# Row normalization on one core: all scaling moved to VectorE, ScalarE left with the stores

## The chip, the cores and the metric

The kernel runs on one core of one Trainium2 chip. The metric is device time in microseconds (us). Before the change it was 317.7 us (median of 3 runs, 317.55 to 318.85). Each run comes with a state: it is slow when it lies over 1.5% above the fastest run of the same kernel. A page of the profile describes one profiled execution; its span is about 2 us shorter than the time of the same run. A ratio of two kernels is the mean time of the one's fast runs over that of the other's of the same rounds, so it is not quite the ratio of the medians that are quoted beside it. An interval is a 95% interval.

## The reference

```python
x: (32, 512, 1024) float32
sums = np.sum(np.abs(x), axis=-1, keepdims=True)
return (x / (sums + 1e-8)).astype(np.float32)
```

There are 16384 rows of 1024 numbers, 67.1 MB in and 67.1 MB out. Each number is read once and written once.

## The kernel before

The rows are cut into ten tiles of 12 rows a partition (6.29 MB each) and one of 8 (4.19 MB). Four buffers of 48 KB a partition rotate, so load 4 (counting from 0) cannot be issued until store 0 has landed. Loads are issued by SyncE, stores by ScalarE. Names are shortened in the cut below.

```python
R = 12
BUFS = 4
...
def normalize(x_tile, r0, k, kv):
    s = stats.tile([P, R], FP32)
    nc.vector.tensor_reduce(out=s[:, :k], in_=x_tile[:, r0 : r0 + k, :],
        axis=X, op=add, apply_absolute_value=True)
    nc.vector.tensor_scalar_add(out=s[:, :k], in0=s[:, :k], scalar1=EPS)
    inv = stats.tile([P, R], FP32)
    nc.vector.reciprocal(out=inv[:, :k], in_=s[:, :k])
    nc.vector.tensor_mul(                      # rows 0 .. kv-1 on VectorE
        out=x_tile[:, r0 : r0 + kv, :], in0=x_tile[:, r0 : r0 + kv, :],
        in1=inv[:, :kv].unsqueeze(2).to_broadcast([P, kv, d]))
    for r in range(kv, k):                     # the other rows on ScalarE
        row = x_tile[:, r0 + r, :]
        nc.scalar.activation(out=row, in_=row, func=Copy, scale=inv[:, r : r + 1])

for i, k in enumerate(rows):
    x_tile = sbuf.tile([P, R, d], FP32)
    nc.sync.dma_start(out=x_tile[:, :k, :], in_=piece(x_flat, i))
    normalize(x_tile, 0, k, k // 2)
    nc.scalar.dma_start(out=piece(out_flat, i), in_=x_tile[:, :k, :])
```

Of the kernel before, what the change touches and what calls it, by code (L numbers as in the profile page):

```python
# [1 line left out]

# [4 lines left out]

FP32 = mybir.dt.float32
EPS = 1e-8


@with_exitstack
def kernel(
    ctx: ExitStack,
    tc: tile.TileContext,
    x: bass.AP,
    out: bass.AP,
):
    nc = tc.nc
    P = nc.NUM_PARTITIONS  # L20

    x_flat = x.flatten_outer_dims()
    out_flat = out.flatten_outer_dims()
    n, d = x_flat.shape


    R = 12
    BUFS = 4
    per_partition = n // P
    assert n % P == 0  # L30
    rows = [R] * (per_partition // R)
    if per_partition % R:
        rows.append(per_partition % R)

    def piece(flat, i):
        a, k = P * sum(rows[:i]), rows[i]
        return flat[a : a + P * k, :].rearrange("(p r) d -> p r d", p=P)

    sbuf = ctx.enter_context(tc.tile_pool(name="sbuf", bufs=BUFS))
    stats = ctx.enter_context(tc.tile_pool(name="stats", bufs=4))  # L40

    def normalize(x_tile, r0, k, kv):

        s = stats.tile([P, R], FP32)
        nc.vector.tensor_reduce(  # L45
            out=s[:, :k],
            in_=x_tile[:, r0 : r0 + k, :],
            axis=mybir.AxisListType.X,
            op=mybir.AluOpType.add,
            apply_absolute_value=True,  # L50
        )
        nc.vector.tensor_scalar_add(out=s[:, :k], in0=s[:, :k], scalar1=EPS)  # L52
        inv = stats.tile([P, R], FP32)
        nc.vector.reciprocal(out=inv[:, :k], in_=s[:, :k])  # L54
        nc.vector.tensor_mul(  # L55
            out=x_tile[:, r0 : r0 + kv, :],
            in0=x_tile[:, r0 : r0 + kv, :],
            in1=inv[:, :kv].unsqueeze(2).to_broadcast([P, kv, d]),
        )
        for r in range(kv, k):  # L60
            row = x_tile[:, r0 + r, :]
            nc.scalar.activation(  # L62
                out=row,
                in_=row,
                func=mybir.ActivationFunctionType.Copy,
                scale=inv[:, r : r + 1],
            )

    with tc.manual_schedule():
        for i, k in enumerate(rows):  # L70
            x_tile = sbuf.tile([P, R, d], FP32)
            nc.sync.dma_start(out=x_tile[:, :k, :], in_=piece(x_flat, i))  # L72
            normalize(x_tile, 0, k, k // 2)
            nc.scalar.dma_start(out=piece(out_flat, i), in_=x_tile[:, :k, :])  # L74


# [1 line left out]
_INS = ['x']  # L78
_OUTS = [((32, 512, 1024), 'float32')]


# [23 lines left out]
```

## Time and profile before

| | before |
|---|---|
| time, median | 317.7 us |
| VectorE (DVE) busy | 212.4 us, 67% |
| ScalarE (ACT) busy | 69.0 us, 22% |
| DMA, mean over the span | 425 GB/s |
| VectorE's wait for loads, all tiles | 81.1 us |

These lines are from the page of the kernel before: the span, the busy time of each engine, and the busy share in 40 equal slices (a digit is tenths, 9 is 90% or more).

```profile
span 315.8 us, 227 instructions
...
DVE 212.4 (67%) x44; ACT 69.0 (22%) x65; POOL 0.2 (0%) x4
...
DVE  0069999998499079719944991797099449949300
...
DMA  8999999999999999999999999999999999999996
```

The reader is to see the row of DMA: it is full in every slice but the first and the last. Nothing that an engine saves can shorten this kernel unless it lets the DMA engines move the same bytes in less time.

The costliest groups of the kernel before (line, engine, operation, tile names, shapes, count; then busy time and mean ns of one; then idle time just before and what ended it):

```profile
L45 DVE TENSOR_REDUCE s<-x_tile 128x12 f32<-128x12288 f32 (+1 forms) x11 | 138.2, 12564 | 81.1 <-DMA x_tile<-in_x_dram 81.1
L62 ACT ACTIVATE x_tile<-x_tile,inv 128x1024 f32<-128x1024 f32 x64 | 67.7, 1135 | 207.6 <-DVE inv L54 207.6
L55 DVE TENSOR_TENSOR x_tile<-x_tile,inv 128x6144 f32<-128x6144 f32 (+1 forms) x11 | 70.0, 6364 | 0.4
```

The multiply is shared about equally: per tile 6.56 us on VectorE beside 6.34 us on ScalarE. VectorE waits 81.1 us for loads, so it has room.

The start of the timeline of the kernel before, merged (start, length, engine, line, operation): tile 0 is multiplied, and its store is issued.

```profile
31.81 6.34 ACT L62 ACTIVATE x_tile<-x_tile,inv 128x1024 f32<-128x1024 f32 x6 [12.13 <-DVE inv L54]
31.81 6.56 DVE L55 TENSOR_TENSOR x_tile<-x_tile,inv 128x6144 f32<-128x6144 f32 x1
38.28 12.95 DVE L45 TENSOR_REDUCE s<-x_tile 128x12 f32<-128x12288 f32 x1
38.45 0.37 ACTq L74 DMA_DIRECT2D out_dram<-x_tile  x1
```

The first store goes out at 38.45 us.

### The profile page before, as it was taken

To read this page: it belongs to the slowest core of one execution; us is meant where nothing else is said; L and a number is where in the kernel's file an instruction comes from. 1 tells how busy PE (TensorE), PEld (TensorE's weight loads), DVE (VectorE), ACT (ScalarE), POOL (GpSimd) and SP (SyncE) were. 2 spreads that over 40 slices of the span, in tenths; PEclk is the share of its full clock that TensorE was granted. 3 is DMA by queue.
4 is the path that set the end of the run, shared out by engine and by line. 5 is a ranking of instruction groups with operands and counts; after the bars stand their busy time and mean duration, and the time that the engine had idled before them with its cause. 6 is when DMAs were issued, how large, how long until landed. Compare 5 with 4: busy or idle time off the path is not lost.

```text
span 315.8 us, 227 instructions
## 1 busy us (share of the span) xinstructions
DVE 212.4 (67%) x44; ACT 69.0 (22%) x65; POOL 0.2 (0%) x4
## 2 busy tenths in 40 slices
DVE  0069999998499079719944991797099449949300
ACT  0010804308007000700440070007003400701300
POOL 0000000000000000000000000000000000000000
DMA  8999999999999999999999999999999999999996
GB/s 311 467 417 411 467 367 442 405 454 430 417 448 430 423 461 423 436 442 417 442 442 411 449 436 411 448 436 423 448 430 436 442 413 450 421 448 417 448 403 278
DMA packets 3169, 134.23 MB, mean 425 GB/s; under 512 B 352, under 2 KB 352, under 8 KB 352
## 3 DMA queue, kind: packets, MB, share of 16 engines
q1 hardware_dynamic: 1584, 67.11, 49.8%
q10 hardware_dynamic: 1584, 67.11, 49.1%
q14 instruction: 1, 0.01, 0.0%
HBM read 67.11 MB, written 67.11 MB: 425 GB/s over the span
## 4 chain that ended last, share of the span: by engine, by line
DMA 55%; DVE 25%; another core or an unknown queue 9%; ACT 4%; issue 0%; SPq 0%; DVEq 0%; ACTq 0%
DMA x_tile<-in_x_dram 41%; DVE s L45 19%; DMA out_dram<-x_tile 14%; DVE x_tile L55 6%; ACT x_tile L62 4%; DVE inv L54 0%; DVE s L52 0%; SPq L72 0%; DVEq L54 0%; ACTq L74 0%
## 5 line engine op out<-in xcount | busy, mean ns | idle before, releaser
L45 DVE TENSOR_REDUCE s<-x_tile 128x12 f32<-128x12288 f32 (+1 forms) x11 | 138.2, 12564 | 81.1 <-DMA x_tile<-in_x_dram 81.1
L62 ACT ACTIVATE x_tile<-x_tile,inv 128x1024 f32<-128x1024 f32 x64 | 67.7, 1135 | 207.6 <-DVE inv L54 207.6
L55 DVE TENSOR_TENSOR x_tile<-x_tile,inv 128x6144 f32<-128x6144 f32 (+1 forms) x11 | 70.0, 6364 | 0.4
L62 ACT ACT_TABLE_LOAD x1 | 1.3, 1283 | 18.4 <-DMA x_tile<-in_x_dram 18.4
L54 DVE RECIPROCAL inv<-s 128x12 f32<-128x12 f32 (+1 forms) x11 | 2.5, 226 | 0.9
L52 DVE TENSOR_SCALAR s<-s 128x12 f32<-128x12 f32 (+1 forms) x11 | 1.9, 173 | 0.4
L89 POOL MEMSET const-bfloat16-1.0<- 128x1 bf16 x1 | 0.1, 101 | 0.0
L89 POOL MEMSET const-uint8-127<- 128x1 uint8 x1 | 0.1, 101 | 0.0
L89 POOL MEMSET const-float32-0.0<- 128x1 f32 x1 | 0.1, 98 | 0.2 <-issue 0.2
L89 POOL MEMSET const-float32-1.0<- 128x1 f32 x1 | 0.1, 98 | 0.0
## 6 DMA issues: line engine op xcount, KB each, us to landing
x_tile<-in_x_dram SPq DMA_DIRECT2D x10, 6144.0 KB, 38.5
out_dram<-x_tile ACTq DMA_DIRECT2D x10, 6144.0 KB, 53.5
x_tile<-in_x_dram SPq DMA_DIRECT2D x1, 4096.0 KB, 33.7
out_dram<-x_tile ACTq DMA_DIRECT2D x1, 4096.0 KB, 19.5
```

Source lines behind the costliest of these rows:

```text
L45: nc.vector.tensor_reduce(out=s[:, :k], in_=x_tile[:, r0 : r0 + k, :], axis=mybir.AxisListType.X, op=mybir.AluOpType.add, apply_absolute_v ...
L52: nc.vector.tensor_scalar_add(out=s[:, :k], in0=s[:, :k], scalar1=EPS)
L54: nc.vector.reciprocal(out=inv[:, :k], in_=s[:, :k])
L55: nc.vector.tensor_mul(out=x_tile[:, r0 : r0 + kv, :], in0=x_tile[:, r0 : r0 + kv, :], in1=inv[:, :kv].unsqueeze(2).to_broadcast([P, kv, d]),)
L62: nc.scalar.activation(out=row, in_=row, func=mybir.ActivationFunctionType.Copy, scale=inv[:, r : r + 1],)
L89: nc = _bacc.Bacc("TRN2", target_bir_lowering=False, num_devices=1)
```

## The change

The intent is to drop the 64 small ScalarE instructions and the uneven split of work: one broadcast multiply per tile on VectorE, and ScalarE only issues stores.

```diff
-    def normalize(x_tile, r0, k, kv):
+    def normalize(x_tile, r0, k):
 ...
         nc.vector.tensor_mul(
-            out=x_tile[:, r0 : r0 + kv, :],
-            in0=x_tile[:, r0 : r0 + kv, :],
-            in1=inv[:, :kv].unsqueeze(2).to_broadcast([P, kv, d]),
+            out=x_tile[:, r0 : r0 + k, :],
+            in0=x_tile[:, r0 : r0 + k, :],
+            in1=inv[:, :k].unsqueeze(2).to_broadcast([P, k, d]),
         )
-        for r in range(kv, k):
-            row = x_tile[:, r0 + r, :]
-            nc.scalar.activation(...)
 ...
-            normalize(x_tile, 0, k, k // 2)
+            normalize(x_tile, 0, k)
```

More of the change, by code (lines that the diff above doesn't have):

```diff
@@ L55, in normalize @@
         nc.vector.tensor_mul(
-            out=x_tile[:, r0 : r0 + kv, :],
-            in0=x_tile[:, r0 : r0 + kv, :],
-            in1=inv[:, :kv].unsqueeze(2).to_broadcast([P, kv, d]),
-        )
-        for r in range(kv, k):
-            row = x_tile[:, r0 + r, :]
-            nc.scalar.activation(
-                out=row,
-                in_=row,
-                func=mybir.ActivationFunctionType.Copy,
-                scale=inv[:, r : r + 1],
-            )
+            out=x_tile[:, r0 : r0 + k, :],
+            in0=x_tile[:, r0 : r0 + k, :],
+            in1=inv[:, :k].unsqueeze(2).to_broadcast([P, k, d]),
+        )
     with tc.manual_schedule():
```

## The prediction

> What bounds the kernel now. The 16 DMA engines. The page's slices show them at 90% or more in every slice but the first and last, 134.23 MB at 425 GB/s over a span of 315.8 us. Loads and stores share them: in the timeline the tile period settles at 29.0 us (reduces begin at 112.19, 141.21, 170.26, ...), and 2 x 6.29 MB in 29.0 us is 434 GB/s. The Trainium skill, "DMA: Bandwidth & Descriptors", section "Where 436 GB/s comes from", gives 435 GB/s as the ceiling for one core; this trace agrees (434). VectorE is busy 67%, ScalarE 22%; VectorE waits 81.1 us for loads (waits view), 8.9 us per tile in the steady part. A store is issued about 53 us before it lands, though 6.29 MB take 29 us at half rate: some 25 us is queueing behind the store before.
>
> What changes. Removed: 64 ACTIVATEs of 1.13 us (67.7 us of ScalarE, 6.34 us per tile, beside VectorE's multiply of 6.56 us) and a hidden table load of 1.28 us. Added: VectorE multiplies 12288 instead of 6144 elements. The trace has 6557 ns for 6144 and 4425 ns for 4096 elements: 1.041 ns an element plus 0.16 us, so an estimated 12.95 us (8.69 us for the last tile), as much as the reduce. The Trainium skill, "VectorE: DVE Perf Modes", section "The perf-mode tier table", has fp32 tensor_tensor at one element a cycle at any size; the two sizes agree. VectorE's period per tile goes from 19.93 us (two unstalled tiles in the timeline) to about 26.35 us.
>
> Critical path. 26.35 is still below the DMA period of 29.0, so the extra 6.4 us per tile should come out of two slacks: VectorE's 8.9 us wait for a load, and the store's queueing. With four buffers a load waits for the store of four tiles ago; that store starts when the store queue reaches it, not when VectorE is done. The end is tight. VectorE begins at 18.35; if it never waits it ends at 18.35 + 10 x 26.35 + 17.9 = about 300 us (295 before). By then about 4 to 5 MB of stores should be left, and the last store (4.19 MB, 9.7 us at 434 GB/s, plus some 2 us to land) ends at about 312 to 316. Laid out by hand at 434 GB/s shared equally, before and after end within 1 us of each other. A VectorE period of 27 us would cost some 2 us, 28 about 12 us: the margin is thin, but the period follows from measured durations.
>
> Predicted: 318.2 us, 8 in 10 between 316.5 and 321.5. Faster by over 2%: 0.02; within 2%: 0.92; slower by over 2%: 0.06.
>
> What would show it. The 12288-element multiply at 12.9 to 13.0 us; VectorE 88 to 90% busy, its idle time before reduces down from 81 us to under 25, mostly the first load; ScalarE with no busy time; DMA still 9 in nearly all slices; median time from a store's issue to landing down from 53 us to 30 to 40; first store issued near 45 us, last near 300 us.
>
> What would make it wrong. The multiply slower than its two sizes say, or slowed by DMA traffic; a gap in the DMA engines near 75 us, when the four loads are done and the fifth waits for the first store; stores issued so late at the end that the engines idle; a time lower by over 2% would mean that DMA was not at its limit.

## More of the kernel before

The end of the kernel before in windows of 10 us (window, its length, busy time of each engine, granted clock, DMA share, GB/s):

```profile
290.00:300.00 10.00, 4.92 (x4) 4.27 (x4) 0.00 (x0) 1.00 1.02 442
300.00:310.00 10.00, 0.00 (x0) 0.00 (x0) 0.00 (x0) 1.00 0.97 419
310.00:320.00 10.00, 0.00 (x0) 0.00 (x0) 0.00 (x0) 1.00 0.28 119
```

The engines stay full until after 310 us and then stop together.

## The result, and the profile after

The changed kernel takes 325.15 us (median of 4 runs, 324.84 to 325.33) against 317.66 us; the ratio is 1.0226 (1.0201 to 1.0252). It is slower by 2.3%, and it lies outside the predicted range of 316.5 to 321.5 us.

The same lines of the changed kernel's page:

```profile
span 323.3 us, 134 instructions
...
DVE 280.2 (87%) x44; POOL 0.2 (0%) x4
...
DVE  0079999999999999999999999999599959999900
...
DMA  8999899999999999999999999999999999999792
...
L45 DVE TENSOR_REDUCE s<-x_tile 128x12 f32<-128x12288 f32 (+1 forms) x11 | 138.2, 12560 | 25.5 <-DMA x_tile<-in_x_dram 25.5
L55 DVE TENSOR_TENSOR x_tile<-x_tile,inv 128x12288 f32<-128x12288 f32 (+1 forms) x11 | 138.3, 12570 | 0.4
```

What VectorE does is nearly as predicted: one multiply costs as much as one reduce, and its wait for loads has shrunk from 81.1 to 25.5 us (under 25 was predicted, and 88 to 90% busy instead of 87). Of the 25.5 us, 18.0 are the first load; the other 7.5 us come late, in front of tiles 7, 8 and 9 (0.78, 3.29 and 3.44 us in the timeline). But for one 8 near 36 us, where the packets followed below show no idle engine, the DMA row has lost digits only at the end.

The timeline at the first store, and the last windows, of the changed kernel (the windows have no ScalarE column, since it is never busy):

```profile
31.49 12.96 DVE L55 TENSOR_TENSOR x_tile<-x_tile,inv 128x12288 f32<-128x12288 f32 x1
44.37 12.95 DVE L45 TENSOR_REDUCE s<-x_tile 128x12 f32<-128x12288 f32 x1
44.48 0.38 ACTq L66 DMA_DIRECT2D out_dram<-x_tile  x1
```

```profile
290.00:300.00 10.00, 9.90 (x4) 0.00 (x0) 1.00 1.06 457
300.00:310.00 10.00, 6.92 (x1) 0.00 (x0) 1.00 0.72 308
310.00:320.00 10.00, 0.00 (x0) 0.00 (x0) 1.00 0.78 336
320.00:325.00 5.00, 0.00 (x0) 0.00 (x0) 1.00 0.03 13
```

The first store is issued at 44.48 us instead of 38.45. At the end the DMA share is 0.72 and 0.78 where before it was 0.97 until the work ran out.

### Looking at the 16 DMA engines one by one

The page gives the mean of the 16 DMA engines. The trace also records each packet (queue, start, duration, bytes) and each engine's report that its part of a DMA has landed. The tables below are worked out from these records. A DMA of 128 partitions is spread over 16 engines, 8 packets of 48 KB each (one partition's run of 12 rows). The records do not name the engine, so I chained packets: one that starts where another ends belongs to the same engine. In the kernel before this gives 16 chains of exactly 176 packets, 88 loads and 88 stores; in the other kernels a few chains swap some packets where two ends coincide.

First and last of the 16 landings of a store, in us from the span's start:

```
                 before                    changed
store   issued  first   last  apart   issued  first   last  apart
0         38.5   70.9   73.6    2.7     44.5   76.1   80.2    4.1
1         58.4   99.9  102.6    2.8     70.8   97.8  106.7    8.9
3        103.4  157.9  160.7    2.8    123.5  157.7  166.0    8.3
6        190.4  244.9  247.6    2.7    202.4  243.0  255.4   12.4
9        277.4  303.5  305.0    1.5    289.2  304.9  312.7    7.8
10       295.2  313.2  314.7    1.5    307.0  317.9  322.4    4.5
```

Before, the 16 engines work in step. In the changed kernel some are up to 12.4 us behind others. The Trainium skill, "DMA: Bandwidth & Descriptors", section "Why a DMA increments its semaphore by 16 and not by 1", states that only the full count of 16 means that all data have landed. This trace agrees: load 10 was issued at 255.5 us, just after store 6's last landing at 255.4, and 12.5 us after its first. So a tile always waits for the slowest engine.

The engines that fall behind are not idle. Nearly every packet takes 1.815 us (27.1 GB/s an engine, 433 GB/s for 16). Some take longer. Call the time over 1.815 us extra. Summed up to the last packet's end and averaged over the engines:

```
                         before   changed   difference
last packet's end         314.2     322.1        +7.8
extra packet time           2.2       4.2        +2.0
idle time of engines        2.7       8.5        +5.8
```

The two differences add up to the whole loss, as they must: an engine has the same bytes to move in both kernels, and is otherwise slow or idle. Until 280 us no engine idles in either kernel except in the first 2 us. The idle time is at the end, where fast engines have nothing left to do: on twelve engines some 3 us before the last store, which VectorE hands over only at 307.0 us, and another 4.4 us between their end at 317.6 us and that of the slowest at 322.1.

Here is where the extra time starts. These are the first packets around store 0 on two engines of the changed kernel. L3.1 is load 3's packet 1, S0.0 is store 0's packet 0; the figure is the duration in us.

```
engine with 25 load packets ahead of its first store packet (4 of 16 engines; 2 look like this, on the other 2 load packets are slow as well):
L3.0 2.51 | S0.0 1.81 | L3.1 1.82 | S0.1 2.10 | L3.2 1.81 | S0.2 2.48 | L3.3 1.81 | S0.3 2.43 | L3.4 1.81 | S0.4 2.47 | L3.5 1.81 | S0.5 2.50 | L3.6 1.81 | S0.6 2.44
engine with 26 load packets ahead (12 of 16 engines):
L3.1 2.76 | S0.0 1.82 | L3.2 1.81 | S0.1 1.81 | L3.3 1.81 | S0.2 1.82 | L3.4 1.81 | S0.3 1.81 | L3.5 1.81 | S0.4 1.81 | L3.6 1.82 | S0.5 1.81
```

Both alternate between a load and a store packet. The Trainium skill, the same page, section "Queues, rings and completion order", states that each engine takes turns between its queues packet by packet, and these lines agree. But on the first engine, where store packet j follows load packet j of tile 3, the store packets take about 2.45 us; on the second, shifted by one packet, none does. In the kernel before, the engines have 22 or 23 load packets ahead, and store packets take 1.81 us on all 16.

### The profile page after: what moved, and what is told of

It reads as the page before. It is cut to its first block, busy times and chain, and to the rows that moved or that the text cites. A ratio compares the mean times of both kernels' runs of the same rounds, so it can differ in the third digit from the quotient of the medians.

```text
span 323.3 us, 134 instructions
## 1 busy us (share of the span) xinstructions
DVE 280.2 (87%) x44; POOL 0.2 (0%) x4
## 4 chain that ended last, share of the span: by engine, by line
DVE 62%; DMA 32%; issue 0%; SPq 0%
DVE x_tile L55 31%; DVE s L45 31%; DMA x_tile<-in_x_dram 17%; DMA out_dram<-x_tile 15%; DVE inv L54 1%; DVE s L52 0%; SPq L64 0%
## 5 line engine op out<-in xcount | busy, mean ns | idle before, releaser
L45 DVE TENSOR_REDUCE s<-x_tile 128x12 f32<-128x12288 f32 (+1 forms) x11 | 138.2, 12560 | 25.5 <-DMA x_tile<-in_x_dram 25.5
L55 DVE TENSOR_TENSOR x_tile<-x_tile,inv 128x12288 f32<-128x12288 f32 (+1 forms) x11 | 138.3, 12570 | 0.4
```

The lines of the kernel that those rows point to most:

```text
L55: nc.vector.tensor_mul(out=x_tile[:, r0 : r0 + k, :], in0=x_tile[:, r0 : r0 + k, :], in1=inv[:, :k].unsqueeze(2).to_broadcast([P, k, d]),)
```

## The experiments

Four theories were on the table at the start. T, mine after reading the traces: loads come late, engines are out of step, and VectorE, having no slack any more, waits. V: only the sum of VectorE's work matters. E: only the later last store matters. D: engines that are out of step cost the time by themselves, whatever VectorE does.

### Which tile matters

`split_first`, `split_middle` and `split_last` are the changed kernel with one tile split as before (tile 0, tile 5, the last). `vector_first` is the kernel before with one tile unsplit.

```diff
# split_first (0), split_middle (5), split_last (len(rows) - 1); the loop before, with
-            normalize(x_tile, 0, k, k // 2)
+            normalize(x_tile, 0, k, k // 2 if i == 0 else k)
# vector_first
+            normalize(x_tile, 0, k, k if i == 0 else k // 2)
```

> Changed kernel, but tile 0 is split between VectorE and ScalarE as before. Theory T (the fifth load waits for a late first store, the 16 DMA engines get out of step, loads come late, and VectorE, which has no slack, waits for them): the first store goes out at 38.5 instead of 44.5 us, stores' landings stay within 3 to 4 us from first to last engine instead of 8 to 12, load 9 lands near 257 instead of 262.7, time 317.5 to 320. Rival V (only the sum of VectorE's work matters): 325.1 minus 6.4, near 318.7, with no change of the landing spreads.

> Changed kernel, but only tile 5 (in the middle) is split. Theory T: VectorE is 6.4 us sooner with tile 5 but then waits for loads 7 to 9, which are as late as before (load 9 lands near 262 to 263); VectorE's waits after the first load rise from 7.5 to about 14 us, the time stays at 324 to 326. Rival V (sum of VectorE's work): near 318.7.

> Changed kernel, but only the last tile (8 rows) is split. It takes VectorE 4.3 us less, all of it after load 9's wait. Theory T: the loads are as late as in the changed kernel (load 9 at 262 to 263), the last store is issued at 302.7 instead of 307.0, time 320.5 to 322.5. Rival E (the whole loss is the later last store, nothing to do with loads): back to within 1 us of 318.

> Kernel before, but tile 0 is multiplied by VectorE alone; all others are split. Theory T: the first store goes out at 44.5, the fifth load has the pause (first packet near 83 to 85 us), and the landings spread as in the changed kernel (5 us or more for stores), yet the time is within 1% of 317.7 because VectorE has 8.9 us of slack a tile: 317.5 to 320. If the spread alone costs time (rival D), 322 or more.

| run | median us | range | ratio to before |
|---|---|---|---|
| split_first | 317.30 | 317.24 to 317.40 | 0.9996 (0.998 to 1.0013) |
| split_middle | 325.35 | 324.18 to 328.40 | 1.0264 (1.021 to 1.0318) |
| split_last | 324.37 | 322.99 to 325.30 | 1.0215 (1.0183 to 1.0246) |
| vector_first | 323.23 | 322.53 to 324.95 | 1.0193 (1.0154 to 1.0232) |

Of `vector_first` the table has the three fast runs; the fourth, 328.76 us, was slow (with it the median is the 324.1 that two later expectations name).

Splitting tile 0 alone gives the whole loss back, with ten of eleven tiles still on VectorE alone. V falls with `split_middle`: 6.4 us less VectorE work in the middle gains nothing. E falls with `split_last`: the last store went out at 302.2 us, 4.8 us sooner than in the changed kernel, and the time fell by only 0.8 us. My expectation of 320.5 to 322.5 was missed as well. The trace shows why: twelve engines end near 314 us, but the four slowest end at 318.7, 320.2, 320.8 and 321.0.

`vector_first` decides against my own theory T. This is the line of its waits that tells of VectorE's slack:

```profile
DVE s L45 <- DMA x_tile<-in_x_dram: 80.3, 8, 18.7
```

VectorE waits 80.3 us for loads, as much as in the kernel before (81.1), and its last store goes out at 300.6 us. The kernel is nevertheless 1.9% slower. Its store landings are 12.7 us apart in the middle of the run. D holds: the loss comes also where VectorE has all its slack.

### When the first store goes out

The next question was what about tile 0 matters: that VectorE did it, or when its store goes out. In `first_vector8` and `first_vector10` tile 0 of the changed kernel has 8 or 10 rows on VectorE and the rest on ScalarE. In `scalar_first` tile 0 of the kernel before is multiplied by ScalarE alone. In `short_first` the changed kernel has the 8-row tile first.

```diff
# first_vector8 (8), first_vector10 (10)
+            normalize(x_tile, 0, k, 8 if i == 0 else k)
# scalar_first (the multiply on VectorE stands under "if kv:")
+            normalize(x_tile, 0, k, 0 if i == 0 else k // 2)
# short_first, on the changed kernel
+    rows = [per_partition % R] + [R] * (per_partition // R)
```

> Changed kernel, but tile 0's multiply is 8 rows on VectorE and 4 on ScalarE, so that the first store goes out near 40.6 us (38.5 with 6 rows, 44.5 with 12). Theory D (what costs is that a first store that comes late leaves a few DMA engines with slow packets and all must wait for them; VectorE's slack is not it). If it is a matter of whether the load queue runs dry before the fifth load can be issued (D1), the store lands near 76 with the loads ending near 79, a margin of 3 us or less: some dry time, time 318 to 321, between the two. If it is the position among load 2's or load 3's packets at which the store comes in (D2), it still comes into load 2: 317 to 318.5, landing spreads under 3 us.

> As first_vector8, but 10 rows on VectorE and 2 on ScalarE: the first store goes out near 42.7 us, its first packet near 47.5, as load 3 begins (46.2). D1: dry time nearly that of the changed kernel, 321 to 325. D2: as in the changed kernel if the packet comes after load 3's first, 323 to 326, else as before, near 318.

> Kernel before, but tile 0 is multiplied by ScalarE alone (12 rows of about 1.06 us after 31.8: first store near 44.5 us); all others are split. VectorE has less work than in the kernel before. Theory D: the same as with tile 0 on VectorE alone, 322 to 326, with landing spreads over 5 us: it is the time of the first store, whichever engine is slow. A theory that needs VectorE's added work: 317 to 318.5.

> Changed kernel (all multiplies on VectorE), but the tile of 8 rows is the first and not the last: the first load lands near 12.5, the first store goes out near 30.5 us, lands near 56, while loads 1 to 3 run until about 70: the load queue never runs dry. VectorE ends near 294 if it never waits. Theory D: landing spreads under 4 us, time 317 to 319.5, though VectorE works as much as in the changed kernel. A theory that VectorE's added work itself costs the time: 323 to 326.

`first_vector8` took 317.66 us (317.38 to 318.12), `first_vector10` 323.31 us (321.82 to 324.87), `scalar_first` 324.25 us (322.95 to 324.69). Two more rows in the first tile, 2.1 us, make the step of 2%. `scalar_first` has less VectorE work than the kernel before and still loses as much: it is the time of the first store, whichever engine is slow. Expectation D1, a gradual loss with a load queue that runs dry, predicted 318 to 321 for `first_vector8` and is not borne out.

`short_first` took 323.51 us (323.27 to 323.84). By the time alone my theory D, which said 317 to 319.5, had failed, and the theory that VectorE's added work costs the time (323 to 326) had won. What D said of the landings came true: those of a store are at most 3.3 us apart, so the engines are in step. The loss is another one, and here VectorE's added work does have a part. The slices of its page:

```profile
DMA  8999999999999999999999999999999999999096
GB/s 326 476 403 434 375 448 428 401 483 397 483 391 446 434 409 470 397 483 391 446 434 434 409 434 440 428 446 415 428 440 434 446 434 440 421 434 421 43 489 293
```

The 0 in the DMA row is a gap near 300 us. The last tile now has 12 rows; store 9 has landed at 300.3 us, VectorE hands over the last tile at 305.0, and all 16 engines are idle for 6 to 7 us. This is an end effect: the last load lands at 278.5 us, and VectorE's reduce and multiply of those 12 rows take the 26.4 us from then on.

### Lateness, position, addresses, and tile size

Two theories were left. L: the later the first store, the worse. P: what counts is where the first store's packets fall among the load's packets. `later_first` is `vector_first` with a needless second reduce of 7 rows of tile 0, which delays the first store to 52.9 us. `out_moved` is the changed kernel with a result that is wrong: tiles of 12 rows are stored in reverse order of tiles, so only the addresses in HBM, the chip's main memory, differ. `r8_b6_vector` is the changed kernel with tiles of 8 rows and 6 buffers, and `short_both` has a 4-row tile at both ends.

```diff
# later_first, on vector_first, in tile 0 only, behind the reduce
+        nc.vector.tensor_reduce(out=again[:, :7], in_=x_tile[:, r0 : r0 + 7, :], ...)
# out_moved
-            nc.scalar.dma_start(out=piece(out_flat, i), ...)
+            nc.scalar.dma_start(out=piece(out_flat, 9 - i if i < 10 else i), ...)
# r8_b6_vector
-    R = 12
-    BUFS = 4
+    R = 8
+    BUFS = 6
# short_both
+    rows = [4] + [R] * 10 + [4]
```

> Kernel before with tile 0 on VectorE alone and, on top, a needless second reduce of 7 rows of tile 0, so that the first store goes out near 52 us, 7.5 us later still than in vector_first (324.1). Its first packet then comes near 57 us, past the middle of load 3, and the load queue is dry for longer. Theory P (position: slow packets arise when the first store's packets run beside the packets of load 3 at the same place in their tiles): the store's first packets meet load 3's last ones, no run of slow store packets between 55 and 80 us, time 317.5 to 320. Theory L (lateness: the later, the worse): 324 or more.

> Changed kernel with a result that is wrong on purpose: the tiles of 12 rows are stored to the output in reverse order of tiles (tile 0's result goes where tile 9's belongs). Timing of VectorE, order of loads and stores, and their places in the on-chip memory are the same; only the addresses of the stores in HBM differ. If the slow packets come of the addresses in HBM of a load and a store at one time (H): gone or much fewer, 317 to 320. If they come of the order of packets or of the on-chip memory (S): as in the changed kernel, 323 to 326.

> Changed kernel (all multiplies on VectorE) with tiles of 8 rows and 6 buffers, the same 192 KB a partition. The first store goes out near 30.1 us, as load 3 begins (near 31), which is the same position as in the changed kernel, but loads 3 to 5 are still queued, so the load queue does not run dry. Theory P: slow store packets in some engines while load 3 runs, landing spreads of 4 us or more, 320 to 324. Theory of the dry queue (D1): no slow packets, 316.5 to 319.

> Changed kernel (all multiplies on VectorE) with tiles of 4, ten times 12, and 4 rows. VectorE begins near 7.5 and ends near 296 us if loads do not hold it, and the last store has 2.1 MB, so the end effect of short_first (7 us in which all 16 DMA engines are idle) should be gone. If the engines stay in step: 316.5 to 319. If store 1's first packets (near 54 us) meet load 4's first ones (near 55) badly: landing spreads over 5 us and 321 to 325.

| run | first store issued | median us | range | widest store landing |
|---|---|---|---|---|
| later_first | 52.9 | 317.65 | 317.20 to 318.65 | 3.7 us |
| out_moved | 44.6 | 324.63 | 324.06 to 325.58 | 12.0 us |
| r8_b6_vector | 30.8 | 317.73 | 317.02 to 318.56 | 2.5 us |
| short_both | 17.7 | 317.98 | 317.54 to 318.10 | 2.4 us |

`later_first` ends theory L. Its first store is 7.7 us later than that of `vector_first`, VectorE does more work, and it is 5.6 us faster. In `out_moved` the time did not improve, so moving the stores to other HBM addresses does not remove the slow packets. `short_both` shows that a short tile at both ends avoids both losses with no row on ScalarE. `r8_b6_vector` came out well where I had expected 320 to 324, because I had expected its packets to fall as in the changed kernel.

### How sharp the position is

In the 12-row runs so far an engine had much extra packet time only where 25 load packets lay ahead of its first store packet, that is, one packet of load 3. `later_first2` puts the first store only 2 us later than `vector_first` did. `r8_b6_first7` and `r8_b6_first6` shift the first store of the 8-row kernel by one and two packets. `vector_later2` is the changed kernel itself with 2.3 us of needless work in tile 0 and nothing else.

```diff
# later_first2: as later_first with :2 and r0 + 2
# r8_b6_first7, r8_b6_first6: R = 8, BUFS = 6, split kernel's normalize
+            normalize(x_tile, 0, k, 7 if i == 0 else k)
# vector_later2: the changed kernel, in tile 0 only, behind the reduce
+        nc.vector.tensor_reduce(out=again[:, :2], in_=x_tile[:, r0 : r0 + 2, :], ...)
```

> As later_first, but the needless reduce covers 2 rows, so that the first store goes out near 47.3 us, only 2.8 us later than in vector_first (324.1). Theory P in its sharp form (an engine is slow when exactly one packet of load 3, that is 25 load packets, lies ahead of its first store packet): all 16 engines have 27 packets ahead or more, packets run at normal length for the 40 us after, time 317.3 to 319.5. Theory L (late first stores cost, and only a store as late as 52.9 escapes): 322 or more.

> r8_b6_vector (317.7), but tile 0 has 7 of its 8 rows on VectorE, so that the first store goes out about 1.1 us, one packet, earlier: 25 or 26 load packets ahead where r8_b6_vector had 26 or 27. Theory P in its sharp form: most engines at 25, with slow store packets for some 20 us, landing spreads over 4 us, time 319 to 322; engines at 26 stay normal. If position alone does not do it with six buffers (the load queue is never dry): 316.5 to 318.5 with normal packets also on engines at 25.

> As r8_b6_first7 with 6 rows on VectorE, the first store one packet earlier again: 24 or 25 load packets ahead. Theory P in its sharp form: slow packets in just the engines at 25; if all are at 24, none and 316.5 to 318. If position does not matter with six buffers: 316.5 to 318.5 with no slow packets anywhere.

> The changed kernel (all multiplies on VectorE) with a needless second reduce of 2 rows of tile 0: 2.3 us more work for VectorE, at the start of the chain that already seemed too long, and the first store goes out near 47 instead of 44.5 us. Theory P (what counts is where the first store's packets fall among load 3's): packets of normal length, store landings spread under 4 us, VectorE ends near 302, time 317.5 to 320, which is faster than the changed kernel by 5 us or more. If VectorE's lack of slack or the lateness of the first store were the cause: 325 to 328.

`later_first2` took 317.79 us (317.64 to 317.95). `vector_later2` took 317.58 us (317.03 to 319.01); its ratio to the kernel before is 1.0 (0.9981 to 1.0018). A kernel with more work than the changed one is 7.6 us faster than it. Its page, its waits and its last windows:

```profile
span 317.1 us, 135 instructions
...
DVE 282.1 (89%) x45; POOL 0.2 (0%) x4
...
DMA  8999999999999999999999999999999999999994
```

```profile
DVE s L45 <- DMA x_tile<-in_x_dram: 18.7, 1, 18.7
```

```profile
290.00:300.00 10.00, 9.90 (x4) 0.00 (x0) 1.00 1.00 433
300.00:310.00 10.00, 1.85 (x1) 0.00 (x0) 1.00 0.97 418
310.00:320.00 10.00, 0.00 (x0) 0.00 (x0) 1.00 0.29 125
```

VectorE waits once, for the first load, and then never again; the DMA windows read as those of the kernel before; store landings are at most 2.9 us apart. The Trainium skill, "SBUF — State Buffer", section "Who interferes with whom", states that DMA does not contend with a compute engine. This run agrees: with VectorE busy 89% of the span, packets take on average 1.4 us of extra time per engine after the first 20 us, against 1.2 us in the kernel before.

All kernels with 12-row tiles and 4 buffers in one table. "Ahead" is the number of load packets in front of an engine's first store packet.

| run | first store issued, us | ahead | engines at 25 | median us |
|---|---|---|---|---|
| before / split_first | 38.5 / 38.5 | 22 to 23 | 0 | 317.7 / 317.30 |
| first_vector8 | 40.5 | 23 to 24 | 0 | 317.66 |
| first_vector10 | 42.6 | 24 to 25 | 10 | 323.31 |
| scalar_first | 44.1 | 25 to 26 | 12 | 324.25 |
| changed | 44.5 | 25 to 26 | 4 | 325.15 |
| out_moved / split_last | 44.6 / 44.7 | 25 to 26 | 3 / 4 | 324.63 / 324.37 |
| split_middle | 44.8 | 25 to 26 | 2 | 325.35 |
| vector_first | 45.2 | 25 to 26 | 2 | 323.23 |
| later_first2 | 47.0 | 26 to 27 | 0 | 317.79 |
| vector_later2 | 47.2 | 26 to 27 | 0 | 317.58 |
| later_first | 52.9 | 29 to 30 | 0 | 317.65 |

In each run with engines at 25 these engines average 3.3 to 5.1 us of extra packet time in the 40 us after their first store packet. The other engines of the table average at most 0.8 us, but for the four at 26 in `scalar_first` (1.8 us) and a single one at 26 in `later_first2` (1.6 us).

The sharp rule does not carry over to 8-row tiles. `r8_b6_first6` took 317.51 us (316.95 to 318.23): 12 of its engines are at 25, and none is slow. `r8_b6_first7` took 324.03 us (323.82 to 324.25): all 16 are at 26, their first store packets take the normal time (1.21 us for 32 KB), and slow packets, mostly of loads, come later (on most of its engines near 133, 172, 212 and 251 us). Its neighbours, with the first store 0.9 us sooner and 0.8 us later, are both fast. So with other tiles a loss of the same size exists, with slow packets too, and is as sensitive to the first store's time, but the position at which it occurs is another one. I had expected 319 to 322 there, too little and for the wrong reason.

What stays open is why a packet becomes slow at such a position. It is not the first store's lateness (`later_first`), the store's HBM addresses as far as one other order of tiles tells (`out_moved`), or VectorE's load (`scalar_first`, `vector_later2`). No run separates the remaining candidates (the places in the on-chip memory, for one, were never changed alone), and I name none as the cause.

No kernel here beats the one before clearly: all that keep the engines in step and the end short lie between 317.3 and 318.0 us.

## Why the prediction was wrong

- **"The 16 DMA engines" bound the kernel.** Right. The medians of all kernels without the loss lie within 0.8 us of each other, whatever VectorE and ScalarE do.
- **"An estimated 12.95 us" for the multiply of 12288 elements, a period of "about 26.35 us".** Right: 12.96 us, and 26.34 us between the starts of the first two reduces (18.03 and 44.37). The Trainium skill, "VectorE: DVE Perf Modes", section "The perf-mode tier table", has fp32 `tensor_tensor` in its slowest mode, and the third size agrees with the first two.
- **"The extra 6.4 us per tile should come out of two slacks."** Right. `split_first` keeps ten full multiplies on VectorE at 317.30 us, and `vector_later2` all of them at 317.58 us.
- **First store "near 45", last "near 300 us".** The first was at 44.5. The last was at 307.0, because VectorE had waited 7.5 us for loads that the slow engines held back. In `vector_later2` it was at 301.9.
- **"Laid out by hand at 434 GB/s shared equally, before and after end within 1 us of each other."** This is the step that failed. It treats the 16 DMA engines as one server with a fixed rate. The runs showed that how long packets take depends on when the first store joins the loads: in the changed kernel four engines got slow packets from about 53 us on (on two of them store packets of about 2.45 instead of 1.81 us), those two ended with over 9 us of extra time, and everything that waits for a whole tile waited for them. The time lost is 2.0 us of extra packet time, averaged over the engines, and 5.8 us in which engines that were ahead had nothing left to do. Why packets are slow after such a start stays open.
- **"A gap in the DMA engines near 75 us" as a risk.** The load queue did run dry there, since load 4 could be issued only at 80.3 us, but the engines were busy with stores. In `later_first` it ran dry as well, for longer, and cost nothing. Of the other risks, "stores issued so late at the end that the engines idle" did come true (some 3 us on twelve engines before the last store), but as a consequence: `split_last` issued that store 4.8 us sooner and gained 0.8 us. None of the risks that I listed was the cause.

The change itself costs nothing in VectorE time. It moved the first store from 38.5 into a window (42.6 to 45.2 us lose, 40.5 and 47.0 us do not) in which this kernel's DMA engines get out of step.

## What to carry to other kernels

In a kernel that DMA bounds, equal bytes do not mean equal time: look at how far apart the 16 engines' landings of one transfer are, because a tile is ready only when the slowest engine is done. If a change that should be free costs 2%, shift the first store by one or two microseconds in either direction, even by needless work, before you blame the engine whose work you changed. Then try the last tile too: a short one keeps the end full when the chain in front of the last store has grown.

## What the Trainium skill lacked or had wrong

- "DMA: Bandwidth & Descriptors" gives a rate per engine and a ceiling, but not that packets of equal size take 1.815 us or 2.4 to 2.5 us depending on when the first store joined the loads; that is worth 2% (317.6 against 323.2 to 325.4 us).
- The same page says that the engines finish independently, but not that those of one core can drift apart and stay so: up to 13.3 us between the first and the last landing of one store (`split_middle`), against 2.8 us in the kernel before.
- The same page, section "Latency and other measured facts", has a first byte after some 0.6 us for transfers issued from SyncE or ScalarE. Here, in the kernel before, the first load's first packet begins 1.0 us after its issue (0.7 to 1.7 us), and the first store's 4.9 us after its issue (38.5 to 43.3 us), behind load packets of 1.8 us each. A store that is issued while loads run starts late.
- No page has the rule at which position packets become slow; with 12-row tiles it was 25 load packets ahead of the first store packet, with 8-row tiles another one, and the reason is open.
